# Projecting the attention's values inside the input projection, ahead of the last group of state-space inputs

## The chip, the cores and the metric

The kernel runs on one core of one Trainium2 chip. The metric is device time in microseconds (us), from the program's start to its end; the median of several runs counts. Five engines work side by side: TensorE (PE: matmuls), VectorE (DVE), ScalarE (ACT: activations, and here also some DMA issues), GpSimd (POOL) and SyncE (SP: DMA issues).

## What is computed

The reference is a two-layer diffusion backbone on 1024 latent and 256 context tokens (1280 in all), model width 1024, in 32-bit floats. The change lies in layer 0. There one input projection gives three things: the low-rank queries `cq` (384) and keys/values `ckv` (256) of a multi-head latent attention, a rotary key (32), and the inputs `s` (512) of a bidirectional state-space layer (S5):

```python
cq, ckv, kr, s = split(u @ w_in)
q = (rms_norm(cq, q_norm) @ w_uq)        # 8 heads x (64 + 32 rotary)
kv = (rms_norm(ckv, kv_norm) @ w_ukv)    # 8 heads x (64 of key, 64 of value)
att = softmax(q k^T * scale) v           # latent rows see all 1280, context rows 256
z = gelu(S5(s) + d_skip * s)             # forward and backward complex scan, state 64
y = concat([att, z * sigmoid(z @ w_glu)]) @ w_out
```

After it come a gated convolutional feed-forward network, an HGRN2 layer and a second feed-forward network; none of these is touched.

## The kernel before

Matrices of 32-bit numbers are split into a high and a low part, and each product is three matmuls (`mm3`, L101 to L105: high by high, low by high, high by low). `split` (L108) makes the two parts: ACT writes the high part (L111), and DVE or GpSimd subtracts it to get the low part (L114). `wload` (L308) loads a piece of weights by SP and splits it, with GpSimd for the low part unless told otherwise. Tokens are handled in blocks `BLK` of 512, 512 and 256.

`in_proj` (L607) computes the projection in pieces of 128 output columns. It does state-space groups 0 and 1, the rotary key, group 2, then the five pieces of `cq` and `ckv` (kept on chip as `cq`, high and low; the last ones in tiles called `late`), and for these the row norms `rs` (L671 and the `rstd` chain on DVE, ending in the copy `rkc`, L679). Then come the last group of state-space inputs, `groups([3])` (L674, matmuls `pin`), two loads of the attention's mask (L675 to L678), and a loop that spreads the norms over rows: 20 transposing matmuls with the identity (L592, `ps`) and DVE copies into `rqk` and `rope` (L686 to L688). The state-space inputs go to DRAM (`Sd`, L627).

`attention` (L694) first projects the values of all heads (L716 to L729): it loads the value columns of `w_ukv` (L718), GpSimd scales them by the norm's gains (L720), they are split, and for each of ten token tiles TensorE runs six matmuls `pv` of 128x512; ACT evicts the result scaled by `rkc` (L728) and issues its store to the DRAM tensor `vd` (L729). The weights and the output tile come from a pool of their own, `vp`, and the results alternate between two PSUM banks.

After this the attention is written as an interleaving of four generators. `qk(h)` (L736) loads the weights of a head (`wqs` L742, `wks` L749) and its values back from `vd` (`vs`, L754), projects keys (`pk`) and queries (`pq`), and finds for every query a bound for its scores (matmuls `pS` L793, maxima `mx` on DVE L796, `pm` L806). `attend(h)` (L810) walks, in each head, 22 tiles of keys against query blocks, 176 tiles in all: three score matmuls `pS`, an exponential on ACT (L821), a split of it into `ph` and `pl` (the subtraction alternates between DVE and GpSimd: 88 `pl` for each), and three matmuls into `po`. `ada_steps` (matmuls `pada`, L257) computes modulation vectors of later stages.

`S5Half.run` (L868) is the state-space layer, in two halves `hh` of 16 groups. For each half: inputs `U` are read back from `Sd` (L874); TensorE forms the state inputs (`pV`, L889, evicted into `H` by ACT, L892); then a scan over 160 chunks: a sweep up of two levels (`bulk`, forward direction on DVE, backward on GpSimd, L908 and L912), 38 sequential steps on GpSimd alone (L931, L933, L934), and a sweep down of the same two levels; then sixteen output steps: four matmuls `pY` against the states and one against the inputs (L950, L953; the profile counts each as two), evicted from one PSUM bank by two ACT instructions (L954, L955), a GELU, and the store to `Zd` (L962). The next stage (`mix_out0`) begins by reading all of `Zd` (L1185).

What sets the order: the program text gives the four generators' weights, but the order of instructions on each engine is made by the scheduler of the tile framework, which simulates a timeline when the kernel is built and lets each engine take what it finds ready; the stage of `in_proj` has priority over what is behind it. On the chip each engine executes its list strictly in that order.

## Time and profile before

| | |
|---|---|
| median of 3 runs | 3795.72 us (3793.88 to 3796.36) |
| the profiled execution's own time | 3789.94 us |
| its span, first to last instruction | 3788.1 us |
| mean granted TensorE clock, of full speed | 0.966 |
| TensorE busy | 3588.2 us, 95% of the span |
| VectorE / ScalarE / GpSimd busy | 2101.3 / 1082.7 / 1178.5 us |

Times of the trace are microseconds from the start of the span. A row of a timeline gives the start, the length, the engine, the line and operation, the output and its inputs, and how many like instructions it stands for ("x8"); a square bracket gives how long the engine had been idle before it, and what released it. A row of a stretch gives for each engine the busy time with the number of instructions, and under PEclk the clock that TensorE was granted, as a share of full speed (1.00 is 2.4 GHz, 0.50 is 1.2 GHz).

### The profile page before, as it was taken

The page shows a single profiled execution, that of the slowest core. Times are in us where ns is not written, and L with a number is a line of the kernel's source. Part 1 is how long each engine was busy: PE and PEld are TensorE (multiplying, and loading weights), DVE is VectorE, ACT ScalarE, POOL GpSimd, SP SyncE. Part 2 cuts the span into 40 slices and gives each one's busy share as a digit, 9 for nine tenths or more (in the row PEclk, how much of TensorE's full clock was granted, in tenths as well). Part 3 has the DMA queues.
Part 4 walks back from the last instruction along what each step waited for, and adds up shares of the span by engine and source line. Part 5 has one row for each costly group of instructions (what it writes and reads, how often), then busy time and mean ns, then how long its engine had stood idle before and what let it go on. Part 6 is the DMA issues. An engine that isn't in the chain of part 4 may idle for free.

```text
span 3788.1 us, 47489 instructions
## 1 busy us (share of the span) xinstructions
PE 3588.2 (95%) x19081; PEld 2910.3 (77%) x19081; DVE 2101.3 (55%) x3294; ACT 1082.7 (29%) x1798; POOL 1178.5 (31%) x1089
## 2 busy tenths in 40 slices
PE   6987899888999999999998999999998999999997
PEld 3764566556788888888887889898987888888885
DVE  7736855784555444444447655565664744545445
ACT  2323445445332121111113322222221511212123
POOL 3627823782442211111114411111122622212122
PEclk9997999988999999999999999999998999999998
DMA  7462345304201111111110210101022111111111
GB/s 243 120 169 73 110 120 141 98 23 146 84 23 34 40 44 40 39 34 34 40 34 29 78 34 29 40 29 40 29 67 89 45 45 45 52 44 51 45 45 45
DMA packets 294301, 243.05 MB, mean 64 GB/s; under 512 B 41214, under 2 KB 255576, under 8 KB 293056
## 3 DMA queue, kind: packets, MB, share of 16 engines
q1 hardware_dynamic: 289152, 227.32, 20.4%
q10 hardware_dynamic: 4928, 12.69, 1.0%
q8 instruction: 150, 2.46, 0.3%
q14 instruction: 71, 0.58, 0.0%
HBM read 203.79 MB, written 38.28 MB: 64 GB/s over the span
## 4 chain that ended last, share of the span: by engine, by line
PE 82%; DVE 7%; POOL 2%; DMA 2%; issue 1%; ACT 1%; SPq 0%; ACTq 0%; POOLq 0%; DVEq 0%
PE pa L105 5%; PE po L103 5%; PE pa L103 5%; PE pa L104 5%; PE po L104 5%; PE po L105 5%; PE pg L103 5%; PE pg L105 5%; PE pg L104 5%; PE ph L104 3%; PE ph L105 3%; PE ph L103 3%; PE pA L1419 3%; PE pmix L103 2%; PE pmix L104 2%; PE pmix L105 2%
## 5 line engine op out<-in xcount | busy, mean ns | idle before, releaser
L114 POOL TENSOR_TENSOR w<-ws,w 128x1024 fp32r<-128x1024 f32 (+1 forms) x205 | 501.1, 2449 | 1570.7 <-ACT w L111 1424.4
L1051 DVE SCALAR_TENSOR_TENSOR acc<-po,mod,acc 128x512 f32<-128x512 f32 (+1 forms) x456 | 309.3, 679 | 559.3 <-PE po L105 559.0
L103 PE MATMUL po<-hh,w 128*128 128x512 f32 (+1 forms) x912 | 342.2, 376 | 11.8 <-DVE acc L1051 10.0
L104 PE MATMUL po<-hl,w 128*128 128x512 f32 (+1 forms) x912 | 335.9, 368 | 5.9 <-DVE hl L114 5.8
L105 PE MATMUL po<-hh,w 128*128 128x512 f32 (+1 forms) x912 | 335.1, 368 | 0.0
L111 ACT ACTIVATE w<-ws 128x1024 fp32r<-128x1024 f32 (+1 forms) x207 | 217.0, 1049 | 409.7 <-PE pg L105 165.3
L103 PE MATMUL pa<-uh,w 128*128 128x512 f32 (+1 forms) x896 | 331.7, 370 | 0.9 <-ACT w L111 0.8
L104 PE MATMUL pa<-ul,w 128*128 128x512 f32 (+1 forms) x896 | 330.2, 369 | 0.1
L105 PE MATMUL pa<-uh,w 128*128 128x512 f32 (+1 forms) x896 | 326.4, 370 | 0.8 <-POOL w L114 0.8
L103 PE MATMUL pg<-uh,w 128*128 128x512 f32 (+1 forms) x872 | 324.2, 372 | 1.9 <-ACT w L111 1.9
L104 PE MATMUL pg<-ul,w 128*128 128x512 f32 (+1 forms) x872 | 322.6, 370 | 0.0
L105 PE MATMUL pg<-uh,w 128*128 128x512 f32 (+1 forms) x872 | 321.5, 372 | 0.6 <-POOL w L114 0.6
L103 PE MATMUL ph<-uh,w 128*128 128x512 f32 (+1 forms) x624 | 238.7, 383 | 1.1 <-ACT uh L1037 1.1
L104 PE MATMUL ph<-ul,w 128*128 128x512 f32 (+1 forms) x624 | 235.1, 377 | 1.5 <-DVE ul L1039 1.5
L105 PE MATMUL ph<-uh,w 128*128 128x512 f32 (+1 forms) x624 | 234.6, 376 | 0.0
L103 PEld LDWEIGHTS po<-hh,w 128*128 128x128 f32 x912 | 173.4, 190 | 46.9 <-DVE acc L1051 12.9
L104 PEld LDWEIGHTS po<-hl,w 128*128 128x128 f32 x912 | 173.9, 191 | 37.9 <-DVE hl L114 6.9
L105 PEld LDWEIGHTS po<-hh,w 128*128 128x128 f32 x912 | 173.8, 191 | 30.2
L103 PEld LDWEIGHTS pa<-uh,w 128*128 128x128 f32 x896 | 168.7, 188 | 32.7 <-ACT w L111 1.0
L105 PEld LDWEIGHTS pa<-uh,w 128*128 128x128 f32 x896 | 168.6, 188 | 32.2 <-POOL w L114 1.3
L104 PEld LDWEIGHTS pa<-ul,w 128*128 128x128 f32 x896 | 168.6, 188 | 32.2 <-DVE ul L1039 0.3
L103 PEld LDWEIGHTS pg<-uh,w 128*128 128x128 f32 x872 | 164.1, 188 | 35.5 <-ACT w L111 2.3
(401 smaller groups left out, 7932.4 us busy)
## 6 DMA issues: line engine op xcount, KB each, us to landing
ws<-in_ffn_w_in_dram SPq DMA_DIRECT2D x88, 512.0 KB
adaw<-in_ada_w_dram SPq DMA_DIRECT2D x80, 512.0 KB
ws<-in_ffn_w_out_dram SPq DMA_DIRECT2D x44, 512.0 KB
ws<-in_hg_w_in_dram SPq DMA_DIRECT2D x40, 512.0 KB
w<-in_ada_w_dram SPq DMA_DIRECT2D x8, 1024.0 KB
ws<-in_ev_w_out_dram SPq DMA_DIRECT2D x10, 512.0 KB
ws<-in_hg_w_out_dram SPq DMA_DIRECT2D x10, 512.0 KB
ws<-in_ev_w_in_dram SPq DMA_DIRECT2D x9, 512.0 KB
```

What stands on the lines that cost most here:

```text
L103: nc.tensor.matmul(ps, lhsT=w[0], rhs=x[0], start=start, stop=False)
L104: nc.tensor.matmul(ps, lhsT=w[0], rhs=x[1], start=False, stop=False)
L105: return nc.tensor.matmul(ps, lhsT=w[1], rhs=x[0], start=False, stop=stop)
L111: nc.scalar.activation(hi, src, AF.Copy)
L114: (nc.gpsimd if elo == "p" else nc.vector).tensor_tensor(lo, src, hi.bitcast(F), op=OP.subtract)
L1051: k.nc.vector.scalar_tensor_tensor(a, ps[:, :e - s], modcol(k, layer, seg, 1 if s >= SEQ else 0, ct), a, op0=OP.mult, op1=OP.add)
L1419: nc.tensor.matmul(ps[:, i * 128:i * 128 + 128], lhsT=km[:, c:c + 128], rhs=raw(Q, c, [[2 * hs, 64 // hs], [SEQ + hs, 2], [1, hs]]), start ...
```

## The change

The projection of the values moves from the head of `attention` into `in_proj`, in front of `groups([3])`; the spreading of the norms and the copy `rkc` come before `groups([3])` too, and the mask's loads stay behind it. The weights `wv` now come from the input projection's own pool, the output tiles from its tag `sq`, and the results rotate over four PSUM banks ("AB") in place of two. Nothing is computed that was not computed before, and each engine has the same number of instructions.

```diff
-    groups([3])
-    for i in range(0, 896, 448):
-        m32 = sp([128, 448], I32, tag="sq", bufs=2)
...
     nc.vector.tensor_copy(k.rkc[:], rs[:, 10:20])
+
+    wkv = A["mla_w_ukv"][0].rearrange("(a p) (h m) -> p a h m", p=128, m=128)
+    gk = k.cols[:, k.at["mla_kv_norm", 0]:][:, 0:2]
+    k.vd = k.tc.dram_tile([T, 512], F, name="vd")
+
+    def srcv(s):
+        for a in range(2):
+            nc.sync.dma_start(out=s[:, a * 512:a * 512 + 512].rearrange("p (h m) -> p h m", h=8), in_=wkv[:, a, :, 64:])
+        v = s[:, :1024].rearrange("p (a m) -> p a m", a=2)
+        nc.gpsimd.tensor_tensor(v, v, gk.unsqueeze(2).to_broadcast([128, 2, 512]), op=OP.mult)
+    wv = wload(k, wp, srcv, 1024)
+    for t in range(10):
+        ps = bank(k, "pv", "AB")
+        for a in range(2):
+            mm3(nc, ps[:], [x[3 + a][:, t * 128:t * 128 + 128] for x in cq], [w[:, a * 512:a * 512 + 512] for w in wv],
+                a == 0, a == 1)
+        o = sp([128, 512], tag="sq", bufs=2)
+        nc.scalar.activation(o[:], ps[:], AF.Copy, scale=k.rkc[:, t:t + 1])
+        nc.scalar.dma_start(out=k.vd[t * 128:t * 128 + 128], in_=o[:])
     k.rqk = M([128, T], tag="rqk")
     for b, (s, e) in enumerate(BLK):
...
+    groups([3])
+    for i in range(0, 896, 448):
+        m32 = sp([128, 448], I32, tag="sq", bufs=2)
+        nc.sync.dma_start(out=m32[:], in_=A["k_mask"][:, i:i + 448])
+        nc.gpsimd.tensor_copy(k.mask[:].rearrange("p l t -> p (l t)")[:, i:i + 448], m32[:])
...
-    vd = k.tc.dram_tile([T, 512], F, name="vd")
+    vd = k.vd
     S5 = S5Half(k, A)
-    vp = Pool(k, "vp")
...
-    wv = wload(k, vp, srcv, 1024, bufs=1, sbufs=1)
...
-        ps = bank(k, "pv", "A")
...
-        o = vp([128, 512], tag="vo", bufs=2)
...
-    vp.free()
```

The last lines left out are those of the added block. From `attention` on, lines of the kernel after have numbers one higher than before (the bulk is L909 and L913, the `pY` L951 and L954).

Since the scheduler makes its lists anew, the change reaches far beyond the lines moved. Three places show it.

TensorE at the end of `in_proj`. Before, the last `pin` of group 3 was followed by the 16 transposes and the value projection, interleaved with the first `pada`:

```order
L103 MATMUL pin<-uh,w 128x256
L104 MATMUL pin<-ul,w 128x256
L105 MATMUL pin<-uh,w 128x256
L592 MATMUL ps<-ident,rs 128x128 x16
L103 MATMUL pv<-w,late_1811 128x512 x2
L257 MATMUL pada<-adaw_2327,sT 32x256 x4
L592 MATMUL ps<-ident,rs 128x128 x4
L104 MATMUL pv<-w,late_1811 128x512
L105 MATMUL pv<-w,late_1813 128x512
```

In the kernel after, the value projection stands behind the last row-norm matmuls `prs`, and the first `pin` of group 3 behind its sixtieth matmul:

```order
L105 MATMUL pin<-uh,w 128x256
L671 MATMUL prs<-ones,rqk 128x1 x4
L103 MATMUL pv<-w,late_1811 128x512
L104 MATMUL pv<-w,late_1811 128x512
L105 MATMUL pv<-w,late_1813 128x512
L103 MATMUL pv<-w,late_1812 128x512
```

```order
L103 MATMUL pv<-w,late_1812 128x512
L104 MATMUL pv<-w,late_1812 128x512
L105 MATMUL pv<-w,late_1814 128x512
L103 MATMUL pin<-uh,w 128x512
L104 MATMUL pin<-ul,w 128x512
L105 MATMUL pin<-uh,w 128x512
```

Behind the last `pin`, TensorE now finds the keys `pk` of head 0 at once; the state-space layer's `pV` of half 0 are spread over the first 17 attend tiles, where all of them stood ahead of the first tile before.

GpSimd at the sweep up of half 0 (`Tm` and `H` are the scan's product and state, `pl` the attention's low part, `wqs` and `wks` weights of a head). Before, it stood among the weights of heads 0 and 1, ahead of any `pl` but one or two:

```order
L908 TENSOR_TENSOR Tm<-Mh,H 128x640
L745 TENSOR_TENSOR wqs<-wqs,cols 128x384
L912 TENSOR_TENSOR H<-H,Tm 128x20x16
L750 TENSOR_TENSOR wks<-wks,cols 128x128
L912 TENSOR_TENSOR H<-H,Tm 128x20x16
L908 TENSOR_TENSOR Tm<-Mh,H 128x640
L912 TENSOR_TENSOR H<-H,Tm 128x20x16 x2
L908 TENSOR_TENSOR Tm<-Mh,H 128x640
L912 TENSOR_TENSOR H<-H,Tm 128x20x16 x2
L908 TENSOR_TENSOR Tm<-Mh,H 128x640
```

After, it stands behind the eighth `pl` and is interleaved with them:

```order
L751 TENSOR_TENSOR wks<-wks,cols 128x128
L114 TENSOR_TENSOR pl<-p,ph 128x512 x3
L909 TENSOR_TENSOR Tm<-Mh,H 128x640
L913 TENSOR_TENSOR H<-H,Tm 128x20x16 x2
L114 TENSOR_TENSOR pl<-p,ph 128x512
L909 TENSOR_TENSOR Tm<-Mh,H 128x640
L913 TENSOR_TENSOR H<-H,Tm 128x20x16 x2
L114 TENSOR_TENSOR pl<-p,ph 128x512
L909 TENSOR_TENSOR Tm<-Mh,H 128x640
L114 TENSOR_TENSOR pl<-p,ph 128x256
L913 TENSOR_TENSOR H<-H,Tm 128x20x16 x2
```

The sequential steps of half 0 moved from `pl` 2 to 14 to `pl` 16 to 29, those of half 1 from `pl` 57 to 70 to `pl` 69 to 85, of 88.

GpSimd at the sweep down of half 1. Before it began (L908) with 18 `pl` still to come, which stand between its pieces:

```order
L934 TENSOR_TENSOR H<-t_5727,H 128x2x16
L908 TENSOR_TENSOR Tm<-Mh,H 128x640
L114 TENSOR_TENSOR pl<-p,ph 128x512
L912 TENSOR_TENSOR H<-H,Tm 128x20x16 x2
L114 TENSOR_TENSOR pl<-p,ph 128x512
L908 TENSOR_TENSOR Tm<-Mh,H 128x640
L114 TENSOR_TENSOR pl<-p,ph 128x512
L912 TENSOR_TENSOR H<-H,Tm 128x20x16 x2
L908 TENSOR_TENSOR Tm<-Mh,H 128x640
L114 TENSOR_TENSOR pl<-p,ph 128x512
L912 TENSOR_TENSOR H<-H,Tm 128x20x16 x2
```

After, three `pl` are left when it begins, and the rest of the sweep has nothing between its pieces:

```order
L935 TENSOR_TENSOR H<-t_5723,H 128x2x16
L909 TENSOR_TENSOR Tm<-Mh,H 128x640
L114 TENSOR_TENSOR pl<-p,ph 128x512
L913 TENSOR_TENSOR H<-H,Tm 128x20x16
L114 TENSOR_TENSOR pl<-p,ph 128x512
L913 TENSOR_TENSOR H<-H,Tm 128x20x16
L114 TENSOR_TENSOR pl<-p,ph 128x256
L909 TENSOR_TENSOR Tm<-Mh,H 128x640
L913 TENSOR_TENSOR H<-H,Tm 128x20x16 x2
L909 TENSOR_TENSOR Tm<-Mh,H 128x640
L913 TENSOR_TENSOR H<-H,Tm 128x20x16 x2
L909 TENSOR_TENSOR Tm<-Mh,H 128x640
```

Accordingly TensorE's sixteen `pY` steps of half 1, ten of which stood among the last attend tiles before, all stand behind the last matmul of the attention (`po`, L829 now):

```order
L826 MATMUL po<-ph,V_2164 128x512
L827 MATMUL po<-ph,V_2165 64x512
L950 MATMUL pY<-H,RO 128x160 x4
L828 MATMUL po<-pl,V_2164 128x512
L826 MATMUL po<-ph,V_2164 128x512
L827 MATMUL po<-ph,V_2165 64x512
L828 MATMUL po<-pl,V_2164 128x512
L103 MATMUL pS<-QT_2160,KT_2156 128x256
```

```order
L827 MATMUL po<-ph,V_2272 128x256
L828 MATMUL po<-ph,V_2273 64x256
L829 MATMUL po<-pl,V_2272 128x256
L827 MATMUL po<-ph,V_2272 128x256
L828 MATMUL po<-ph,V_2273 64x256
L829 MATMUL po<-pl,V_2272 128x256
L951 MATMUL pY<-H,RO 128x160 x4
L954 MATMUL pY<-U,Tm 128x160
L951 MATMUL pY<-H,RO 128x160 x4
L954 MATMUL pY<-U,Tm 128x160
```

On SP the loads of head 0's weights and values now stand directly behind `in_proj`, ahead of the store of group 3 and the loads of `U`; before they stood behind these. From the next stage (`mix_out0`) on, the lists are practically the same.

## Rows read from the trace of the kernel before

**Rows 1.** The page: busy time of TensorE, share of the span, instructions.
```profile
PE 3588.2 (95%) x19081; PEld 2910.3 (77%) x19081; DVE 2101.3 (55%) x3294; ACT 1082.7 (29%) x1798; POOL 1178.5 (31%) x1089
```

**Rows 2.** Stretches of the span: length, busy time by engine, PEclk, DMA share, GB/s.
```profile
core 0: us, PE busy (x) PEld busy (x) DVE busy (x) ACT busy (x) POOL busy (x), PEclk, DMA share, GB/s
293.00:343.00 50.00, 25.97 (x103) 14.55 (x101) 43.20 (x53) 9.09 (x19) 39.11 (x39) 0.64 0.13 29
423.00:480.00 57.00, 46.83 (x236) 28.54 (x234) 54.73 (x79) 21.33 (x41) 50.01 (x37) 0.91 0.32 93
667.00:731.00 64.00, 52.30 (x266) 32.03 (x264) 58.59 (x72) 24.68 (x48) 44.66 (x29) 0.87 0.34 99
731.00:802.00 71.00, 69.01 (x358) 46.39 (x355) 47.18 (x80) 39.49 (x72) 61.02 (x130) 0.98 0.20 59
802.00:853.00 51.00, 35.66 (x125) 24.87 (x124) 48.27 (x55) 16.41 (x31) 41.47 (x26) 0.77 0.06 17
906.00:922.00 16.00, 12.62 (x53) 9.68 (x52) 2.10 (x5) 4.11 (x15) 0.00 (x0) 0.75 0.60 182
343.00:906.00 563.00, 519.23 (x2711) 340.81 (x2707) 389.92 (x580) 277.72 (x543) 330.74 (x430) 0.94 0.36 100
```

**Rows 3.** Timeline of TensorE, 234 to 343 us: start, length, instruction, idle before.
```profile
235.63 0.28 PE L105 MATMUL pin<-uh,w 128*128 128x256 f32 x1
235.75 1.95 PE L592 MATMUL ps<-ident,rs 128*128 128x128 f32 x16
255.82 0.39 PE L103 MATMUL pv<-w,late 128*128 128x512 f32 x1
256.05 0.39 PE L104 MATMUL pv<-w,late 128*128 128x512 f32 x1
...
293.86 0.69 PE L103 MATMUL pk<-late,wk 128*64 128x512 f32 x1 [0.73 <-ACT wk L111]
...
300.15 0.76 PE L889 MATMUL pV<-U,RO 128*64 128x160 f32 x8
...
340.81 0.80 PE L104 MATMUL pS<-QT,KT 97*128 97x512 f32 x1 [11.59 <-DVE QT L114]
```

**Rows 4.** Timeline of SyncE, its DMA issues at 286 us.
```profile
286.10 1.28 SPq L742 DMA_DIRECT2D wqs<-in_mla_w_uq_dram  x1
```

**Rows 5.** The exponentials of the attention, first and last start.
```profile
L821 ACT ACTIVATE p<-pS x176: 361/597/602, 343.4 to 902.0; 128x512 f32<-128x512 f32 x160, 128x256 f32<-128x256 f32 x16
```

**Rows 6.** Timeline of GpSimd in the scans, 322 to 849 us.
```profile
322.16 2.02 POOL L908 TENSOR_TENSOR Tm<-Mh,H 128x640 f32<-128x640 f32 x1
...
327.33 2.02 POOL L908 TENSOR_TENSOR Tm<-Mh,H 128x640 f32<-128x640 f32 x1
...
796.46 1.29 POOL L114 TENSOR_TENSOR pl<-p,ph 128x512 fp32r<-128x512 f32 x1 [0.43 <-PE po L828]
...
800.07 0.35 POOL L931 TENSOR_TENSOR t<-Mh,H 128x64 f32<-128x64 f32 x1
...
801.19 0.36 POOL L931 TENSOR_TENSOR t<-Mh,H 128x64 f32<-128x64 f32 x1
...
844.29 1.87 POOL L908 TENSOR_TENSOR Tm<-Mh,H 128x640 f32<-128x640 f32 x1
...
848.67 1.87 POOL L908 TENSOR_TENSOR Tm<-Mh,H 128x640 f32<-128x640 f32 x1
```

**Rows 7.** Timeline of TensorE at the end of the stage, 907 to 931 us.
```profile
907.09 1.35 PE L950 MATMUL pY<-H,RO 64*128 64x160 f32 x8 [0.59 <-ACT zt L955]
...
909.50 1.35 PE L950 MATMUL pY<-H,RO 64*128 64x160 f32 x8 [0.59 <-ACT zt L955]
...
914.31 2.50 PE L950 MATMUL pY<-H,RO 64*128 64x160 f32 x8 [0.59 <-ACT zt L955]
...
918.23 2.50 PE L950 MATMUL pY<-H,RO 64*128 64x160 f32 x8 [0.59 <-ACT zt L955]
920.65 0.90 PE L953 MATMUL pY<-U,Tm 128*128 128x160 f32 x2
```

More of the change, by code (lines that the diff above doesn't have):

```diff
@@ L673, in in_proj @@
             rstd(k, sp, rs[:, i * 10:i * 10 + 10], pc[:, 0:10], 10, (1.0 / 384, 1.0 / 256)[i], "rs")
-    groups([3])
-    for i in range(0, 896, 448):
-        m32 = sp([128, 448], I32, tag="sq", bufs=2)
-        nc.sync.dma_start(out=m32[:], in_=A["k_mask"][:, i:i + 448])
-        nc.gpsimd.tensor_copy(k.mask[:].rearrange("p l t -> p (l t)")[:, i:i + 448], m32[:])
-    nc.vector.tensor_copy(k.rkc[:], rs[:, 10:20])
+    nc.vector.tensor_copy(k.rkc[:], rs[:, 10:20])
+    wkv = A["mla_w_ukv"][0].rearrange("(a p) (h m) -> p a h m", p=128, m=128)
[15 more added lines that the diff above has]
+        nc.scalar.dma_start(out=k.vd[t * 128:t * 128 + 128], in_=o[:])
     k.rqk = M([128, T], tag="rqk")
@@ L709, in attention @@
     gk = k.cols[:, k.at["mla_kv_norm", 0]:][:, 0:2]
-    vd = k.tc.dram_tile([T, 512], F, name="vd")
+    vd = k.vd
     S5 = S5Half(k, A)
-    vp = Pool(k, "vp")
-    def srcv(s):
-        for a in range(2):
-            nc.sync.dma_start(out=s[:, a * 512:a * 512 + 512].rearrange("p (h m) -> p h m", h=8), in_=wkv[:, a, :, 64:])
-        v = s[:, :1024].rearrange("p (a m) -> p a m", a=2)
-        nc.gpsimd.tensor_tensor(v, v, gk.unsqueeze(2).to_broadcast([128, 2, 512]), op=OP.mult)
-    wv = wload(k, vp, srcv, 1024, bufs=1, sbufs=1)
-    for t in range(10):
-        ps = bank(k, "pv", "A")
-        for a in range(2):
-            mm3(nc, ps[:], [x[3 + a][:, t * 128:t * 128 + 128] for x in cq], [w[:, a * 512:a * 512 + 512] for w in wv],
-                a == 0, a == 1)
-        o = vp([128, 512], tag="vo", bufs=2)
-        nc.scalar.activation(o[:], ps[:], AF.Copy, scale=k.rkc[:, t:t + 1])
-        nc.scalar.dma_start(out=vd[t * 128:t * 128 + 128], in_=o[:])
-    vp.free()
     PP = Pool(k, "attp", "right")
```

## The prediction

> **What bounds the kernel now.** The page comes first: TensorE is busy for 95% of the span [rows 1], so what is left to gain or lose is a few stretches in which it waits. I looked for these in the table of stretches, then read the timelines of TensorE, GpSimd and SyncE at their edges. They all lie in the stage that the change touches. From the last `pin` at 235.6 [rows 3] to the first exponential of the attention at 343.4 [rows 5], 107.5 us go by in which TensorE projects the values (14 us of matmuls), forms half 0's `pV`, and otherwise waits; from 293 to 343 it is busy for 26 of 50 us, at a clock of 0.64 [rows 2]. In the attention it is busy for 519 of 563 us [rows 2]; the 44 us lost lie where GpSimd's scan holds up the attention's `pl`: sweep down of half 0 (423 to 480), sweep up and down of half 1 (667 to 731, 802 to 853). At the end stands a chain: sequential steps end at 802, sweep down to 853, sixteen `pY` steps to 921.6 [rows 7], then the next stage, which needs all of them. In the kernel before ten of the sixteen steps are done when the attention ends at 906, so that only 16 us stick out.
>
> **Step 1, the projection in its new place.** Sixty matmuls at a pitch of 0.235 us (255.82 to 256.05 [rows 3]) are 14.0 us; twenty transposes at 1.95/16 = 0.12 us [rows 3] are 2.4 us. Both are now on TensorE's path ahead of group 3, and the last `pin` ends that much later than 235.9. New waits: the scaling of the weights stands on GpSimd, queued behind it there is the low part of a weight piece; the loads (two on SP) stand in front of group 3's weights; the transposes and the evictions by `rkc` wait for the norm chain, which before ran beside group 3. Their bounds: nothing, if the matmuls in front last longer than the chain, and some 4 us if TensorE stands for it. I take 2, as the sixty matmuls cover a norm chain that needs no longer than the 16 transposes waited for before. `in_proj` ends at 235.9 + 14.0 + 2.4 + 2 = 254.5.
>
> **Step 2, the opening of the attention.** What was removed from here is the value projection and, by the new order, the whole first part of S5 (`pV`, sweep up). Before, the first load of head 0's weights was issued at 286.1 [rows 4], `pk` began 7.8 us later, at 293.9, and the first exponential came 49.5 us after that. Of these 49.5, 11.6 were a wait for `QT`, which stood on DVE among the sweep up [rows 3], and TensorE was busy for 26 us of them, at a clock of 0.64 [rows 2], `pV` of half 0 included; I take off 24, as if nearly all its waits went, and keep 25.5. In the kernel after, the loads stand directly behind `in_proj`: 7.8 + 25.5 = 33 us, bounds 31 to 36 (and up to 49 if the low clock and the waits for DVE stay). First exponential at 254.5 + 33 = 287.5, which is 56 us earlier than before.
>
> **Step 3, from there to the end of the sequential steps of half 1.** This is where the gain can be lost, because the scan work that stood ahead of the attention now stands inside it. Going by stretches of before [rows 2]: sixteen tiles ahead of the first sweep up, with `pV` between, 45 us of matmuls, say 52; the sweep up of half 0, now among `pl`, as that of half 1 before, 62 to 64; its sequential steps, 70 to 74 (38 steps at 1.12 us are 43 us [rows 6], and 13 to 16 `pl` at 1.29 us and more, each with waits, lie between); the sweep down of half 0, now with four `pl` in place of eight, 46 (57 before); the middle with no scan, 187 (480 to 667); the sweep up of half 1, 62; its sequential steps with 16 `pl`, 74. Sum 556, so that these end at 287.5 + 556 = 843. Counted by TensorE's work instead: 519 us of before's stretch, less ten `pY` steps at 1.8 us (their pitch of 2.41 without the gap of 0.59 [rows 7], 18) and the last six tiles (an estimate from 519/176 = 2.9 us a tile, the last ones being small: 14), plus half 0's `pV` (16 groups at 0.76 [rows 3], 12), is 499; with the 44 us of waits of before 543, so 830. I take 838, against 802 before.
>
> **Step 4, the end.** With the sequential steps at 838 the attention has six tiles left, where before it had 36. The sweep down has six pieces on GpSimd. The first has the last three `pl` in between, some 10 us; five at the pitch of 5.1 us that such pieces have with DVE at work beside them (322.16 to 327.33), or 4.4 as at the end of before (844.29 to 848.67 [rows 6]): 32 to 35.5 in all, 35.5 taken. Then 1.5 us each for the two `Tm` loads, of which the second is partly hidden, 3 us. Then sixteen `pY` steps with nothing else on TensorE. Their pitch was 2.41 us at the full clock (907.09 to 909.50) and 3.92 us at half clock (914.31 to 918.23 [rows 7]): 38.6 or 62.7 us. TensorE has by then waited for over 20 us. Before, such `pY` steps by themselves lost the full clock at 914 and did not regain it in 7 us; from 293 to 343 the clock was mostly low too. So it begins low, and I take 3.4 on average: 54.4. In sum 35.5 + 3 + 54.4 = 93 us, bounds 74 to 101, all of it exposed. `pY` ends at 838 + 93 = 931, against 921.6: **9.5 us later**. Behind that the lists are the same as before, so the rest keeps its length. The profiled execution had 3789.94 us of its own, 3799.5 then; the median of the runs lies 5.8 above it, so 3795.7 + 9.5 = **3805 us**.
>
> Weighed against the skill: the pitch of the `pY` steps is the term of step 4 that depends on the clock. The rows show the clock falling from 2.41 to 3.92 us a step although no gap between matmuls there was longer than 0.6 us. The Trainium skill, page "TensorE: Matmul & The Clock Gate", section "HAM oscillation — how this bites in real kernels", puts a fallen clock down to a pause of the engine; by it such steps, which never pause for long, would run at the full clock once they had got it. The trace disagrees, and its row decides.
>
> **Rivals.** *Full clock at the end.* If `pY` runs at 2.41 us soon after its start, the tail is 35.5 + 3 + 38.6 = 77, and `pY` ends at 915, 6.5 us earlier than before: 3789, no measurable change by a bound of 0.2% (7.6 us, about what a measurement of this kernel can tell from no change). For it: the steps at 907 to 912. Against it: the fall at 914. The page named above would give this time.
> *Faster.* Stretches of the scan in which TensorE was not short of work take no longer than the work itself; with the count by TensorE's work, and a sweep up of half 0 that costs less than that of half 1, the sequential steps end at 820 to 828 and `pY` at 913 to 921: 3777 to 3795. It decides below 828, where the mean tail breaks even (828 + 93 = 921). For it: the count gave 830. Against it: the stretches from 667 to 853 were each long for GpSimd's sake, not TensorE's.
> *Much slower.* The sum by stretches holds (843) and all of the tail is at half clock (101): 944, 22.5 us later, 3818. For it: every stretch is as measured. To this side also goes the opening at 49 us in place of 25.5, which adds up to 15.
> *The change doesn't shorten the opening*: if head 0's weights or the `adaw` transfers of the modulation come late, or DVE's work for `rope` stands in front of the `tq` of head 0, `attend` starts 15 us later and all follows: 3820. Against it: SP issues these loads ahead of `U` and the store of group 3.
>
> **How the numbers follow.** Forecast (3799 to 3811) 0.30; full clock at the end 0.20, faster 0.22; much slower 0.16, late opening 0.12. Faster by over 0.2% (under 3788): most of the rival "faster" and a little of the full clock, 0.22. Within 0.2%: the rest of those two and the forecast's lower part, 0.28. Slower: the forecast's upper part and the last two, 0.50. The range holds 8 in 10 from 3783 to 3826: the lower end leaves out the better half of "faster", the upper end a late opening with a slow tail.
>
> **What would show it.** Step 1: `pv` at a pitch of 0.235 us behind `prs`, the last `pin` ending at 253 to 256. Step 2: the first exponential at 285 to 292. Step 3: the last sequential step of half 1 at 829 to 843; if the stretches in which GpSimd sweeps are 46 and 62 us long, the sum by stretches was right, if 35 to 55, the count by work. Step 4: last `po` some 10 us after it, then some 25 us of GpSimd with TensorE idle, then sixteen `pY` steps at 2.41 or 3.92 us, the last near 931, and the granted clock there at 0.5 to 0.8. Wrong would be: a first exponential after 300, `pY` among the attention's last tiles, or a difference in time behind `pY`.

## The result

The kernel after takes 3837.59 us (median; 3835.19 to 3842.40) against 3794.8 us before (3793.74 to 3796.36): a ratio of 1.0118, 95% interval 1.0106 to 1.0131. It is 43 us slower, where 9.5 us slower was forecast and 3826 was the upper end of the range. The profiled execution has a span of 3836.4 us.

The page of the kernel after, the row of all engines' busy times (as [rows 1]), and its table of stretches (as [rows 2]; length, busy time by engine, PEclk, DMA share, GB/s):

```profile
PE 3605.1 (94%) x19081; PEld 2920.7 (76%) x19081; DVE 2097.8 (55%) x3294; ACT 1081.7 (28%) x1798; POOL 1177.7 (31%) x1089
```

```profile
360.00:418.00 58.00, 48.71 (x245) 29.44 (x238) 54.14 (x70) 22.64 (x42) 44.72 (x36) 0.85 0.36 103
...
490.00:536.00 46.00, 31.18 (x131) 17.25 (x130) 42.52 (x48) 11.72 (x22) 33.41 (x24) 0.72 0.27 80
...
733.00:793.00 60.00, 47.12 (x226) 30.97 (x223) 55.50 (x70) 24.60 (x46) 44.24 (x28) 0.86 0.17 50
793.00:868.00 75.00, 66.19 (x288) 45.77 (x286) 46.57 (x69) 43.92 (x80) 67.00 (x131) 0.98 0.15 42
868.00:914.00 46.00, 10.92 (x34) 7.11 (x32) 19.82 (x25) 5.49 (x12) 37.62 (x23) 0.59 0.25 73
914.00:976.00 62.00, 50.85 (x152) 39.41 (x152) 6.91 (x15) 11.26 (x39) 0.00 (x0) 0.50 0.19 53
```

The last two rows are the loss: for 108 us after the sequential steps TensorE has 62 us of work at most, first waiting for GpSimd's sweep, then in `pY` at half clock. Before, only the 16 us of [rows 2] from 906 to 922 stood alone. The sweeps and sequential steps themselves (58, 46, 60 and 75 us) are nearly as long as the prediction took them from the stretches of before (62 to 64, 46, 62 and 74).

The exponentials of the attention (as [rows 5]) begin 36 us earlier than before:

```profile
L822 ACT ACTIVATE p<-pS x176: 360/597/602, 307.2 to 887.9; 128x512 f32<-128x512 f32 x160, 128x256 f32<-128x256 f32 x16
```

and TensorE's timeline at the end (as [rows 7]) runs 54 us longer:

```profile
910.25 1.43 PE L951 MATMUL pY<-H,RO 64*128 64x160 f32 x4 [11.53 <-POOL H L913]
914.28 0.90 PE L954 MATMUL pY<-U,Tm 128*128 128x160 f32 x2 [2.60 <-DMA Tm<-s5T]
915.77 2.50 PE L951 MATMUL pY<-H,RO 64*128 64x160 f32 x8 [0.59 <-ACT zt L956]
...
919.68 2.50 PE L951 MATMUL pY<-H,RO 64*128 64x160 f32 x8 [0.59 <-ACT zt L956]
...
974.51 0.90 PE L954 MATMUL pY<-U,Tm 128*128 128x160 f32 x2
...
984.13 1.22 PE L103 MATMUL pglu<-zs,w 128*128 128x512 f32 x2 [8.72 <-ACT zs L1206]
```

The last `pY` ends at 975.4 (921.6 before), and the first `pglu` of the next stage starts at 984.1 (930.3 before), 8.7 us behind the last `pY` in both. Behind that the stages differ by a few us only: span less the last `pY` is 2866.5 us before and 2861.0 after.

So the attention started 36 us earlier and ended 15 us earlier, while the state-space layer, which shares the stage, ended 54 us later.

### The profile page after: what moved, and what is told of

It reads as the page before. It is cut to its first block, busy times and chain, and to the rows that moved or that the text cites. A ratio compares the mean times of both kernels' runs of the same rounds, so it can differ in the third digit from the quotient of the medians.

```text
span 3836.4 us, 47507 instructions
## 1 busy us (share of the span) xinstructions
PE 3605.1 (94%) x19081; PEld 2920.7 (76%) x19081; DVE 2097.8 (55%) x3294; ACT 1081.7 (28%) x1798; POOL 1177.7 (31%) x1089
## 4 chain that ended last, share of the span: by engine, by line
PE 81%; DVE 6%; POOL 4%; DMA 2%; issue 1%; ACT 1%; SPq 0%; ACTq 0%; POOLq 0%; DVEq 0%
PE pa L105 5%; PE pa L103 5%; PE pa L104 5%; PE po L103 5%; PE pg L103 5%; PE pg L105 5%; PE po L104 5%; PE po L105 5%; PE pg L104 5%; PE ph L104 3%; PE ph L105 3%; PE ph L103 3%; PE pA L1420 3%; PE pmix L103 2%; PE pmix L105 2%; PE pmix L104 2%
## 5 line engine op out<-in xcount | busy, mean ns | idle before, releaser
L104 PE MATMUL po<-hl,w 128*128 128x512 f32 (+1 forms) x912 | 335.9, 368 | 5.8 <-DVE hl L114 5.8
L104 PE MATMUL pa<-ul,w 128*128 128x512 f32 (+1 forms) x896 | 330.4, 369 | 0.1
L104 PEld LDWEIGHTS pa<-ul,w 128*128 128x128 f32 x896 | 168.6, 188 | 32.2 <-DVE ul L1040 0.4
L105 PEld LDWEIGHTS pa<-uh,w 128*128 128x128 f32 x896 | 168.6, 188 | 32.1 <-POOL w L114 1.3
```

Of the source, the lines that this page charges most:

```text
L104: nc.tensor.matmul(ps, lhsT=w[0], rhs=x[1], start=False, stop=False)
L105: return nc.tensor.matmul(ps, lhsT=w[1], rhs=x[0], start=False, stop=stop)
```

## Two theories

**S5 chain.** The stage ends with the later of two things, the attention or the state-space layer's serial chain (loads of `U`, `pV` of half 0, sweep up, sequential steps, sweep down, `pY`, and the same for half 1, whose `U` and `H` share half 0's buffers). In the kernel before the chain already ends last, 15 us behind the attention (922 and 906). The change starts the chain later and puts it beside the attention from its first step; what the attention gains is worth nothing.

**The place.** The projection's time in the input projection, and the later group 3, are what is lost, by themselves.

In the runs below two numbers are read from each trace: where the attention ends (start of its last eviction `ao`) and where the chain ends (end of the last `pY`). The evictions, first and last start, in the kernel before and in the kernel after:

```profile
L833 ACT ACTIVATE ao<-po x24: 360/576/595, 375.6 to 906.3; 65x512 f32<-65x512 f32 x16, 65x256 f32<-65x256 f32 x8
```

```profile
L834 ACT ACTIVATE ao<-po x24: 362/590/597, 342.4 to 891.7; 65x512 f32<-65x512 f32 x16, 65x256 f32<-65x256 f32 x8
```

Times are medians; ratios are against the kernel before, run on the same chip in turns. The experiments ran on several chips, on which the kernel before took 3790.9 to 3794.8 us, so two experiments are best compared by their ratios. A trace is of one execution, and differences of 1 to 3 us between two traces can be chance (with the same input projection the last `pin` ends at 257.3 to 260.0 in five kernels).

In the edits, `S` is the generator of the state-space layer, `A1` that of the modulation; `some(n, S)` takes its next n steps, so that they stand earlier in the program text. `behind(k, x)` holds what it encloses back in the lists until instruction `x` has been issued. `bank` takes the PSUM banks that its letters stand for, in turn; `k.banks` says which these are.

## Experiment 1: half 0's pV ahead of the keys again

```diff
+    for _ in some(8, S):
+        pass
     for _ in zip_longest(qk(0), some(8, A1)):
...
-            with behind(k, k.pace):
+            with behind(k, k.pace if h else k.formed):
...
-                            nc.tensor.matmul(ps[64 * q:64 * q + 64, i * 160:i * 160 + 160],
+                            k.formed = nc.tensor.matmul(ps[64 * q:64 * q + 64, i * 160:i * 160 + 160],
```

> The kernel after, with one thing put back as it was before: half 0's pV stand ahead of head 0's keys on TensorE, so that the sweep up of half 0 comes ahead of the attention's first tile again. The projection stays in front of group 3. Theory 'S5 chain': the end of the stage is set by the state-space layer's serial chain, and the kernel after loses because that chain starts later and runs beside the attention from its first step on. Then the chain has before's length again from a start some 24 us later, no pY is left behind the last po, and the time is 3780 to 3805 (30 to 55 us less than the kernel after), although the first exponential comes 30 to 40 us later than in the kernel after. Rival 'the place': the projection's 19 us in the input projection and the later store of group 3 are what is lost; then the time stays at 3825 or more.

3804.05 us, ratio 1.0033 (1.0021 to 1.0045). The first exponential comes at 361.5, 54 us later than in the kernel after (30 to 40 were expected), and the kernel is 34 us faster. TensorE's last rows of the stage, attention and `pY`:

```profile
928.39 0.54 PE L956 MATMUL pY<-U,Tm 128*128 128x160 f32 x2
...
937.12 0.41 PE L829 MATMUL po<-pl,V 128*128 128x256 f32 x1
```

The chain ends at 928.9 and is covered; now the attention is last. One matmul order takes back about three quarters of the loss (34 of 43 us by the medians, 32 by the ratios) with the projection left in front of group 3.

How the chain won is not quite as expected. Its first `pV` is still 15.6 us later than in the kernel before (276.7 against 261.1), but half 0's `pV` then take 33 us, where they took 45 in the kernel before and 66, spread over the attend tiles, in the kernel after. The first sequential step is at 351.1, 2 us earlier than in the kernel before (353.1) and 67 us earlier than in the kernel after (417.9).

## Experiment 2: the projection behind group 3

```diff
+    groups([3])
+    for i in range(0, 896, 448):
...
     nc.vector.tensor_copy(k.rkc[:], rs[:, 10:20])
...
-    groups([3])
-    for i in range(0, 896, 448):
...
     sp.free()
```

> The kernel after, with the projection and the spreading of the norms behind group 3 and the mask, still inside the input projection. Theory 'S5 chain': the loads of U wait for the end of the input projection either way, and the attention's first tiles still run ahead of the sweep up; all sixteen pY of half 1 still follow the last po; 3825 to 3845, like the kernel after. Rival 'the place': group 3 is projected and stored some 18 us earlier, the chain starts that much earlier, and the time falls to 3805 to 3822.

3818.02 us, ratio 1.0078 (1.0057 to 1.0100): in the range of 'the place' and below that of 'S5 chain', though all sixteen `pY` still follow the last `po`. The place is worth 20 us by the medians, 15 by the ratios. What the place in front of group 3 costs is seen on SyncE. In the kernel after, its queue waited 10 us for the last `pin`, whose end frees the room of head 0's weights (SyncE's waits, 259 to 295 us; in all, times, longest):

```profile
SPq L743 <- PE pin L105: 10.0, 1, 10.0
```

and everything behind it, head 0's weights, `adaw` and `U` (issued from 264.4 to 279.9), was then loaded with little for TensorE to do: from 260.0 to 286.4 it stood for 7.9 and 9.2 us. With group 3 first, the last `pin` ends at 238.1, and head 0's weights and the store of group 3 go out while TensorE projects the values (238 to 256). `U` still goes out behind the projection, but earlier, and its eight loads are issued in 9 us in place of 16:

```profile
238.03 0.38 SPq L743 DMA_DIRECT2D wqs<-in_mla_w_uq_dram  x1
...
241.02 0.34 SPq L627 DMA_DIRECT2D Sd<-sTt  x1
...
257.95 9.03 SPq L875 DMA_DIRECT2D U<-Sd  x8
```

`pk` follows the projection at once (255.9), the first exponential is at 292.4 (307.2), the first `pV` at 276.9 (291.1), and the chain ends at 951.7, 24 us earlier than in the kernel after. Behind group 3 the projection is cover for the loads of head 0's weights; in front of group 3 it covers none of the loads that wait for the last `pin`.

## Experiment 3: the kernel before, with the chain held back

```diff
-        merge((24, attend(h)), *([(20, qk(h + 1))] if h < 7 else []), *([(34, some(34, S)), (12, some(12, A1))]))
+        merge((24, attend(h)), *([(20, qk(h + 1))] if h < 7 else []), *([(34, some(34 if h > 1 else 0, S)), (12, some(12, A1))]))
```

> The kernel before, with the state-space layer held back in the program text during heads 0 and 1; the projection stays where it was. In the lists half 0's start is unchanged, but its pY and the pV of half 1 fall later, the sweep up of half 1 begins 8 pl (16 tiles) later, and 78 of the 80 pY matmuls of half 1 stand behind the last po in place of 36. Theory 'S5 chain': this alone makes the kernel slower by 20 to 45 us (3815 to 3840), with nothing of the projection moved. Rival 'the place': within 8 us of the kernel before.

3839.73 us, ratio 1.0131 (1.0112 to 1.0150), as slow as the kernel after, with nothing of the projection moved. The first exponential is where it was (344.0) and the attention ends at 910.9 (906.3). The chain's last row:

```profile
969.18 0.90 PE L953 MATMUL pY<-U,Tm 128*128 128x160 f32 x2
```

The loss of the kernel after can thus be had from the chain alone.

## Experiment 4: two PSUM banks for pY

```diff
-                    ps = bank(k, "pY", "D")
+                    ps = bank(k, "pY", "DF")
...
-        k.banks = dict(BANKS, B="2", C="345")
+        k.banks = dict(BANKS, B="2", C="34", F="5")
```

> The kernel after, with two PSUM banks in turn for pY in place of one (the second taken from the three of the keys' and queries' projection). In the lists half 1's pY end in head 6, ahead of the last 40 tiles. Theory 'S5 chain': with the chain off the end, the early start of the attention counts at last: from the first exponential at about 307 some 575 to 590 us of a stage bound by TensorE, the next stage 30 us earlier than in the kernel before, 3755 to 3775, which would be faster than the kernel before. Rival 'the place', or the attention's own cost beside the scan: no better than the kernel before, 3795 or more.

3828.66 us, ratio 1.0103 (1.0084 to 1.0122): the expected gain of 60 to 80 us didn't come. The chain did leave the end (last `pY` at 865.2), but the attention now lasts until 961.9. The bank was taken from the keys and queries, and their maxima hold TensorE up (its waits from 640 to 960; in all, times, longest):

```profile
PE pS L794 <- DVE mx L797: 15.3, 11, 4.5
PE pq L103 <- DVE mx L797: 9.1, 4, 4.3
```

In the kernel before the same two waits come to 0.8 and 1.9 us from 480 to 906. The run says nothing against the later of two ends; it moved the other end.

## Experiment 5: the tail's matmuls done twice

```diff
-                    for d in range(2):
-                        for i in range(2):
+                    for r in range(1 + hh):
+                        for d in range(2):
+                            for i in range(2):
...
-                                             start=d == 0 and i == 0, stop=False)
+                                                 start=d == 0 and i == 0, stop=r < hh and d == 1 and i == 1)
```

> The kernel after with the four matmuls against the states in each pY step of half 1 done twice (the second time counts, the output is the same). Every list is otherwise that of the kernel after. It asks whether the half clock in the tail hangs on how little TensorE has to do between the hand-overs: in the kernel after fifteen of sixteen steps have a pitch of 3.92 us at half clock, against 2.41 at full clock in the kernel before. Theory 'the gaps keep the clock down': with twice the work the full clock comes back within some steps, the pitch is about 0.59 + 2 x 1.28 + 0.54 = 3.7 us, and the time is that of the kernel after within 12 us although TensorE does more. Rival 'the clock stays down for the whole tail whatever is done': the pitch is 3.92 + 2.43 = 6.3 us, 39 us more, 3870 to 3880.

3863.91 us, ratio 1.0185 (1.0169 to 1.0200), 26 us above the kernel after, 6 us short of the range of 'the clock stays down'. The clock stays down for the whole tail (TensorE's timeline, and the stretch of the tail):

```profile
914.83 4.63 PE L952 MATMUL pY<-H,RO 64*128 64x160 f32 x16 [0.59 <-ACT zt L957]
919.39 0.90 PE L955 MATMUL pY<-U,Tm 128*128 128x160 f32 x2
920.88 4.63 PE L952 MATMUL pY<-H,RO 64*128 64x160 f32 x16 [0.59 <-ACT zt L957]
```

```profile
913.00:1005.00 92.00, 82.82 (x272) 71.45 (x272) 6.89 (x14) 10.77 (x37) 0.00 (x0) 0.50 0.13 36
```

The pitch is 6.05 us (6.3 and 3.7 were the two forecasts), with the same gap of 0.59. The theory that too little work kept the clock down falls at this amount of work; whether the gap itself does, no run shows.

## Experiments 6 to 8: the chain off the end, in three kernels

All three: two banks in turn for `pY`, the second taken from `pada`, which shares the three banks of the keys and queries; on the kernel before (6), after (7), and with the projection behind group 3 (8).

```diff
-                    ps = bank(k, "pY", "D")
+                    ps = bank(k, "pY", "DF")
...
-        k.banks = dict(BANKS, B="2", C="345")
+        k.banks = dict(BANKS, B="2", C="345", E="345", F="7")
```

> The kernel before, with two PSUM banks in turn for pY; the second is the one that pada had, and pada takes its turns in the three banks of the keys' and queries' projection. In the lists half 1's pY end in head 4, so the state-space chain is off the end. If the end of the stage is the later of the chain's and the attention's end, only the attention is left: it starts at 343 as before, has 11 us more of pY in it and ends 10 to 20 us later than before's 906, and the next stage follows at once: 3780 to 3800, about the kernel before. If pada in the shared banks holds up the keys and queries as the missing bank did in the run with two banks for pY, 3805 or more.

> The same change of banks on the kernel after. In the lists half 0's pV now stand ahead of the first attend tile, and half 1's pY end in head 5. Theory 'the later of two ends': the chain is off the end, the attention starts at 305 to 325 and ends 20 to 35 us earlier than in the run that does the same to the kernel before: 3755 to 3775. Rival 'the projection's place costs by itself': no faster than that run.

> The same change of banks with the projection behind group 3 in the input projection. In the run that moved it there, head 0's weights were loaded while TensorE projected the values, and the first exponential came 15 us earlier than in the kernel after. If that cover is what the place in front of group 3 gives away, this run is 10 to 18 us faster than the one with the projection in front of group 3 and the same banks; if not, the two are within 5 us of each other.

3892.15, 3867.90 and 3869.83 us; ratios 1.0260 (1.0244 to 1.0275), 1.0192 (1.0177 to 1.0207) and 1.0199 (1.0177 to 1.0221). As a remedy this is bad: the attention stretches to 1024, 1000 and 1001, waiting on TensorE for `pada`'s loads among other things (19.3 us in the first of them). The times forecast for 6 and 7 were missed by 90 us and more; in 6 its own rival (3805 or more) came true. As a comparison they tell the theories apart. The chain ends between 820 and 835 in all three, 165 to 204 us ahead of the attention's end, and there the kernel with the moved projection is **24 us faster**, where 20 to 35 had been expected: the change's sign hangs on which end is last. Not all of the 24 is the earlier start. The first exponential is 11 us earlier (335.9 against 346.9), and 13 us more come behind it; the lists differ there too, and TensorE's `pS` and `pq` wait 26 us for the maxima `mx` in 6 and 6 us in 7. Expectation 8 missed: behind group 3 the first exponential was 5 us earlier (330.4 against 335.9), and that was lost again by the end, so the place alone is worth nothing here.

## Experiment 9: behind group 3, and half 0's pV first

The edits of experiments 1 and 2 together.

> The projection behind group 3 in the input projection, and half 0's pV ahead of head 0's keys on TensorE: both edits that each took back a part of the loss. With the attention first, the place behind group 3 was worth 20 us. If that is a cost of the place by itself (loads that lose their cover), it is worth 15 to 20 us here too, and the time is 3785 to 3792. If it works through the start of the state-space chain alone, it is worth what the chain's first loads gain: they waited for the end of the input projection in both, U was issued at 258 against 260.5, so 2 to 5 us, and the time is 3799 to 3804.

3796.84 us, ratio 1.0010 (1.0001 to 1.0019). The place is worth 7 us here (9 by the ratios), between the two expectations, where it was worth 15 to 20 with the attention first. The first `pV` comes at 268.0 (276.7 with the projection in front), the attention ends at 929.8 (938.3). Nearly all of the loss is back, and nothing is won over the kernel before. The two edits gave back 34 and 20 us alone and give back 41 together.

## Experiment 10: behind group 3, attend tiles held until the sweep

```diff
+    for _ in some(16, S):
+        pass
     for _ in zip_longest(qk(0), some(8, A1)):
...
-                k.pace = mm3(nc, ps[:, :n], [x[0:97, t * 128:t * 128 + 128] for x in kk_], [x[0:97, s:e] for x in q], True, True)
+                with behind(k, None if h else k.formed):
+                    k.pace = mm3(nc, ps[:, :n], [x[0:97, t * 128:t * 128 + 128] for x in kk_], [x[0:97, s:e] for x in q], True, True)
...
+                with behind(k, None if h else k.swept):
...
```

(on the kernel of experiment 2; `k.formed` is half 0's last `pV`, `k.swept` the last step of its sweep up on GpSimd)

> The projection behind group 3; head 0's keys, queries and maxima go first, its attend tiles wait on TensorE for half 0's last pV, and their pl on GpSimd for the sweep up of half 0. So the sweep has GpSimd and VectorE to itself and the opening of the attention still runs while U is loaded. In the lists 45 of the 80 pY of half 1 stand behind the last po (36 in the kernel before, all 80 in the kernel after). If the later of the two ends sets the stage, this is the kernel before moved forward by some 5 to 15 us at the first exponential, and given back some of it in the tail: 3780 to 3795, level with the kernel before or a little faster. If the projection's place costs by itself, 3805 or more.

3790.97 us, ratio 0.9994 (0.9983 to 1.0004): level with the kernel before. Its exponentials, and its last `pY`:

```profile
L823 ACT ACTIVATE p<-pS x176: 364/597/608, 307.5 to 887.8; 128x512 f32<-128x512 f32 x160, 128x256 f32<-128x256 f32 x16
```

```profile
921.96 0.90 PE L960 MATMUL pY<-U,Tm 128*128 128x160 f32 x2
```

The attention starts where it does in the kernel after (307.2) and the chain ends where it does in the kernel before (921.6), and the time is that of the kernel before. This is the plainest of the runs: an attention that starts 36 us earlier and ends 10 us earlier (895.9 against 906.3) is worth nothing while the chain ends last.

## Experiment 11: the spreading of the norms alone

```diff
-    groups([3])
...
     nc.vector.tensor_copy(k.rkc[:], rs[:, 10:20])
     k.rqk = M([128, T], tag="rqk")
...
+    groups([3])
```

> The kernel before with one part of the change alone: the spreading of the norms and the copy rkc stand in front of group 3, the projection of the values stays in the attention. TensorE does 2.4 us of transposes earlier, the lists are nearly those of the kernel before (30 of 80 pY of half 1 behind the last po, 36 before). Both theories: within 6 us of the kernel before, so that the loss belongs to the projection of the values.

3798.90 us, ratio 1.0019 (1.0009 to 1.0028), 6 us slower, at the edge of what was expected: the last `pin` ends 3 us later, the first `pV` comes 3 us later (264.0), the chain ends at 933.0. So some 6 of the 43 us can go with the spreading, and the rest belongs to the projection of the values.

## Experiment 12: a second buffer in the chain of the kernel before

```diff
-                x = W([128, 512], tag="rc")
+                x = W([128, 512], tag="tq", bufs=2)
...
-                t = P([128, 2, 160], tag="zt", bufs=1)
+                t = P([128, 2, 160], tag="zt", bufs=2)
```

> The kernel before with a second buffer for zt, the tile through which a pY step's GELU goes (its room comes from a scratch tile of the queries that now shares the ring of tq). Nothing of the projection is moved. It shortens the state-space chain where it is handed over between ScalarE and VectorE: in the lists 20 of the 80 pY of half 1 stand behind the last po in place of 36. If the chain's end sets the stage, 3 to 10 us less than the kernel before; if not, within 3 us.

**3780.24 us, ratio 0.9963 (0.9950 to 0.9975)**: 12 us faster than the kernel before (3 to 10 were expected), and the fastest of all. The attention starts as before (343.1); the chain ends at 911.9:

```profile
907.50 0.28 PE L828 MATMUL po<-pl,V 128*128 128x256 f32 x1
...
911.40 0.54 PE L953 MATMUL pY<-U,Tm 128*128 128x160 f32 x2
```

How it got shorter isn't as expected: half 0's `pY` take 121 us as before (119). Half 1's sequential steps start 11 us earlier (721.0 against 731.9), since `pV` and the sweep up in front of them are shorter in the new lists. That the chain's end was the lever is shown, that the buffer's hand-over was isn't.

## All runs in one table

Ends in us of the trace; "later" is the later of the two ends.

| kernel | first pV | first exponential | attention ends | chain ends | span | span less later |
|---|---|---|---|---|---|---|
| before | 261.1 | 343.4 | 906.3 | **921.6** | 3788.1 | 2866.5 |
| after | 291.1 | 307.2 | 891.7 | **975.4** | 3836.4 | 2861.0 |
| 1, pV first | 276.7 | 361.5 | **938.3** | 928.9 | 3802.7 | 2864.4 |
| 2, behind group 3 | 276.9 | 292.4 | 863.0 | **951.7** | 3814.7 | 2863.0 |
| 3, before, chain late | 261.0 | 344.0 | 910.9 | **970.1** | 3836.0 | 2865.9 |
| 4, two banks for pY | 285.5 | 309.3 | **961.9** | 865.2 | 3826.6 | 2864.7 |
| 5, tail twice | 288.8 | 303.7 | 886.7 | **1005.0** | 3861.9 | 2856.9 |
| 6, before, banks | 260.9 | 346.9 | **1024.4** | 820.3 | 3889.2 | 2864.8 |
| 7, after, banks | 285.0 | 335.9 | **1000.0** | 835.1 | 3866.6 | 2866.6 |
| 8, behind, banks | 277.2 | 330.4 | **1001.4** | 825.6 | 3865.2 | 2863.8 |
| 9, behind, pV first | 268.0 | 352.4 | **929.8** | 922.8 | 3798.0 | 2868.2 |
| 10, behind, held | 271.8 | 307.5 | 895.9 | **922.9** | 3787.3 | 2864.4 |
| 11, spreading alone | 264.0 | 339.2 | 921.4 | **933.0** | 3797.3 | 2864.3 |
| 12, before, zt | 260.8 | 343.1 | 908.5 | **911.9** | 3777.9 | 2866.0 |

The last column stays within 2857 to 2868 while the later end moves over 112 us, whichever of the two it is. Both theories had a part: the later end, which in the kernels before and after is the chain's, sets the time, and the place in front of group 3 is one of the things that delay it. (By the traces 30 of half 1's 80 `pY` matmuls stand behind the last `po` in the kernel before, 75 in experiment 3, and 40, 20 and 10 in experiments 10, 11 and 12; the numbers in the expectations are 3 to 10 too high.)

For the kernel after the chain's 54 us come apart as follows, each from the two traces. The first `pV`, in the kernel before and in the kernel after:

```profile
261.10 0.76 PE L889 MATMUL pV<-U,RO 128*64 128x160 f32 x8 [2.81 <-DMA vd<-vo]
```

```profile
291.11 1.34 PE L890 MATMUL pV<-U,RO 128*64 128x160 f32 x8
```

It is 30.0 us later: `in_proj` ends 24 us later (260.0 against 235.9), and the loads of `U` and `RO` stand on SyncE among those of head 0 and `adaw`: the eight issues of `U` take from 264.4 to 279.9, where they took from 240.7 to 250.5. From the first `pV` to the first sequential step it is 126.7 us in place of 92.0, 35 us more: `pV` and sweep up now run beside the attention's first tiles, and half 0's last `pV` ends at 357.3, 2 us ahead of the sweep up. From there to the end of half 1's sequential steps 1 us more in all (450.0 against 448.5). The tail, from there to the last `pY`, is 12 us shorter (107.6 against 119.9). The first two shares aren't independent: in experiment 1 the first `pV` was 15.6 us late as well, and with `pV` ahead of the tiles none of that was left at the first sequential step.

## Why the prediction was wrong

The mechanism and the sign were right (the chain's tail, exposed behind an attention that ends early). The size was out by 44 us in the last `pY` (975.4, forecast 931), and each of the four steps had a term too small, the opening and the tail most of all:

**Step 1, +5.5.** The last `pin` ends at 260.0, not 254.5. The sixty `pv` have the forecast pitch (0.235), and TensorE stood for the norms for 1.64 us. Two things were missed. The profile counts each of the twenty transposes as two (40 in the trace), so 1.95/16 was the price of half a one; in the kernel after they take some 4.4 us in place of 2.4. And GpSimd's scaling of the weights (1.89 us, from 168.6 on, with the set-up of the state-space layer queued behind it) delays that set-up: its next piece starts at 171.1, against 168.8 before (0.7 us of this were there earlier), and the first row-norm matmul comes at 191.2, 3.9 us late. The step had named GpSimd's queue, but priced only the wait at the end. Part of it is chance: in the four other kernels with this input projection (experiments 1, 4, 5 and 7) the last `pin` ends at 257.3 to 259.3.

**Step 2, +14.2.** The first load of head 0 to `pk` is 8.0 us (forecast 7.8). From `pk` to the first exponential it is 39.3 us, where 25.5 was kept; TensorE's clock there is 0.68:

```profile
267.90 0.69 PE L103 MATMUL pk<-late,wk 128*64 128x512 f32 x1 [7.89 <-ACT wk L111]
...
286.36 1.08 PE L257 MATMUL pada<-adaw,sT 128*32 128x256 f32 x8 [9.22 <-DMA adaw<-in_ada_w_dram]
```

```profile
268.00:307.00 39.00, 29.78 (x160) 17.29 (x161) 19.86 (x31) 9.04 (x17) 12.15 (x25) 0.68 0.88 178
```

The step took off nearly all waits of the old opening and put no new one in. But `pada` stands among head 0's queries and waits 9.2 us for its weights, which were loaded under the value projection before; for the other 30 us TensorE is busy. The whole opening, 47 us, lies above the bounds of 31 to 36 and within the 49 that the step gave for a low clock. The first exponential, at 307.2, is past the 300 that was to show the prediction wrong. The late `adaw` was a rival, at 0.12, and it came together with 'much slower', at 0.16. The text of 'much slower' allowed for this with up to 15 us more, but the chances were added as for alternatives, and the range left out both at once.

**Step 3, +10.1.** From the first exponential to the last sequential step it is 560.6 us. The sum by stretches said 556; the count by TensorE's work, 543, was wrong, and taking a value between the two (550.5) gave away what the rows had right. In these stretches the scan's engines are busy nearly throughout: VectorE for 54 of 58, 43 of 46 and 56 of 60 us in the sweeps, GpSimd for 67 of 75 us in the steps. The stretch in the middle, with no scan, took some 10 us more than the 187 of the sum. The rival 'faster' rested on the count by work; its lower end, 3777, doesn't follow from its own terms either, as `pY` at 913 would be 3787.

**Step 4, +14.6.** The tail is 107.6 us, above the upper bound of 101. The sweep takes 41.7 in place of 35.5. Its first piece was not some 10 us but 21, for one `pl` that took 10.39 (GpSimd's timeline; the five pieces behind it have 4.1 each, less than the 5.1 taken):

```profile
877.48 10.39 POOL L114 TENSOR_TENSOR pl<-p,ph 128x512 fp32r<-128x512 f32 x1 [3.33 <-PE po L829]
...
889.75 1.88 POOL L909 TENSOR_TENSOR Tm<-Mh,H 128x640 f32<-128x640 f32 x1
...
893.86 1.85 POOL L909 TENSOR_TENSOR Tm<-Mh,H 128x640 f32<-128x640 f32 x1
```

That `pl` is of this execution: in experiment 5, with the same order on GpSimd, it took 1.42 us, three of the five pieces behind it had the 5.1, and the sweep took 37.1 us, 1.6 more than forecast. Then 4.0 us for the first step's weights, and 61.1 for the sixteen `pY`, all at half clock (0.50 in the stretch from 914), where a mean of 3.4 us a step had been taken for a clock that would come back (54.4). The rows at hand, 914 to 921 in [rows 7], said half clock; nothing said that it would come back. The rival with the full clock falls: in 61 us, and 92 in experiment 5, with no gap above 1.5 us, the clock did not rise. With it falls the time that the Trainium skill, page "TensorE: Matmul & The Clock Gate", section "HAM oscillation — how this bites in real kernels", would give.

**What the steps left out** is not the path: half 0's `pV` and the sweep up did hang on the attention's tiles, as the sum had it (sweep up at 359.3, 52.1 us behind the first exponential, where 52 was taken). It is what the matmuls that move had hidden in their old place. There the projection stood beside the loads of `U`, `RO` and `adaw`. In front of group 3 it covers none of them; with `pV` ahead of the keys (experiment 1) TensorE stands for them openly:

```profile
276.72 1.34 PE L892 MATMUL pV<-U,RO 128*64 128x160 f32 x8 [19.45 <-DMA RO<-s5R]
```

The text priced the matmuls that move and named no work that they had hidden.

## What to carry to other kernels

Where two chains share a stage, find out which ends last and follow the change along that one: starting the other earlier is worth nothing (experiment 10), and delaying the last one costs in full (experiment 3). Work that waits for little, such as the projection here, can be worth most at a boundary between stages, where it covers the loads that need the freed room: 15 to 20 us in experiment 2, 7 to 9 in experiment 9, nothing in experiment 8, where the other chain ended last. If a scheduler makes the order, a move in one place can cost most through what it lets run first elsewhere; pin that order (experiment 1) before judging the move.

## What the runs showed of the hardware

A subtraction on GpSimd that takes 1.29 us as a rule took 10.39 in the kernel after (above), from 877.5 to 887.9. In that time VectorE ran sixteen operations without a break, the sweep's but for one, the last of them until 888.4:

```profile
876.42 1.10 DVE L909 TENSOR_TENSOR RO<-Mh,H 128x512 f32<-128x512 f32 x1
...
885.68 2.68 DVE L913 TENSOR_TENSOR H<-H,RO 128x256 f32<-128x256 f32 x3
```

The longest `pl` of the kernel before is 2.66 us. In other kernels such a `pl` took 5.89 (experiment 3), 4.82 (experiment 8) and 4.44 us (experiment 1), each with VectorE at work without a break, mostly on the scan's operations. In experiment 5, where GpSimd has the order of the kernel after, the same `pl` was done in 1.42, and VectorE's operations beside it took longer instead (1.96 us for two that took 0.92 in the kernel after, 1.87 for one that took 1.07). The `pl` of experiment 5 and that of experiment 3:

```profile
878.78 1.42 POOL L114 TENSOR_TENSOR pl<-p,ph 128x512 fp32r<-128x512 f32 x1 [3.33 <-PE po L829]
```

```profile
444.59 5.89 POOL L114 TENSOR_TENSOR pl<-p,ph 128x512 fp32r<-128x512 f32 x1 [1.26 <-PE po L828]
```

The Trainium skill, page "SBUF — State Buffer", section "SBUF: two separate sides", says that VectorE, for operations with two inputs from SBUF, and GpSimd, when it reads SBUF, take turns by an exclusive lock on a shared pair of ports, held for a whole instruction. The rows agree with a GpSimd instruction that finds the ports taken again and again, through sixteen instructions at the most seen here, and with a winner that differs from run to run; no run varies this alone, so that the lock is the cause isn't shown.

TensorE's clock, once at 1.2 GHz (granted clock 0.50) at the head of the tail, stayed there through 61 us of `pY` with gaps of 0.59 us and one of 1.47, and through 92 us with twice the matmuls against the states between the same gaps (experiment 5). In the kernel before it fell at 914 among such steps [rows 7], with no gap above 0.59 us since 853.
